# First layer's variance summed with tokens on partitions, its inverse root taken on four columns and spread by a product with a scaled identity

## The chip, the cores and the metric

The kernel runs on one core of a Trainium2 chip. A core has TensorE (matmuls, with the loads of their stationary operand shown apart as PEld), VectorE (DVE), ScalarE (ACT) and GpSimd (POOL); the queue of SyncE (SP) issues all of this kernel's transfers. The metric is the device time of one execution in microseconds (us), as the median of several runs.

## The reference, cut to what matters

Two layers over 1024 tokens of 1024 channels. The change lies in the first one, a convolution module:

```python
h = x @ w_in + b_in
a, a_gate, z = split(h, 3)
u = conv(a * sigmoid(a_gate), width 31, causal, per channel) + b_dw
u = silu(layer_norm(u, ln_g, ln_b))        # over the channels of a token
y = (u * silu(z)) @ w_out + b_out
x = layer_norm(alpha * x + y, g, b)
```

Here `layer_norm` subtracts the mean over the 1024 channels, and multiplies by `rsqrt(var + 1e-5)`, with one variance for each token. The second layer is a dilated sliding-window attention over 16 heads in three groups, with an output projection and a norm of the same kind.

## The kernel before

The kernel is written as steps, each with an engine, a cost, a priority, the steps that it comes after, and buffers that it takes and frees. A planner (`Order.run`) simulates the engines with these costs, takes on each engine the ready step of the smallest priority, and writes all instructions in the order that comes out; each engine then works its own list strictly in that order. So a changed cost can change the written order of every engine from there on, the attention's too.

In the first layer channels lie on the partitions. A tile is 128 channels by 512 tokens; there are eight chunks of channels (0 to 7) and two halves of the tokens (0 and 1). TensorE computes the projections `pa`, `pg` and `pz` (line 300) as three products of split operands. The convolution (`conv`) is a chain of 31 taps for each chunk and half: ScalarE multiplies and GpSimd adds some ten of them (lines 428 and 432, through the tiles `cvt` in the rings `tb0` and `tb1` of two buffers each), VectorE does the others (line 444). VectorE's order is given by `DVE_ORDER`: `c` and `d` are the convolution of half 0 and half 1, `s` is a half's sums (`stats`), `m` what follows them (`apply`).

```python
DVE_ORDER = "c0d0 c1c2 d1c3 c4d2 c5c6 d3c7 s0 m0 d4d5 d6d7 s1 m1".split()
```

`stats` works on one half. The mean over channels is a product with `ones`, a 128x128 matrix whose elements are all 1/1024, so that each partition of the bank `mp` holds the same row of 512 means (line 469). VectorE subtracts it in place (line 483), ScalarE squares (line 488), GpSimd adds some squares in pairs (line 495), and TensorE sums them into the bank `vp`, again with `ones` (line 503): four sums in half 0 (`SUMS` is 8, all in pairs), six in half 1. ScalarE takes the root (line 519) and VectorE the reciprocal (line 523), both on 128x512 and in place. `apply` multiplies each chunk by the result (line 535), and goes on with the activation (line 539), the gate (line 545) and the split for the output projection (lines 550 and 555). The splits of the weights are steps of ScalarE (`whi`, line 241) and of GpSimd or VectorE (`wlo`, line 250), with two buffers each.

The output projection `po` (line 655) takes half 0 and then half 1. What it gives is normalized, turned by TensorE (`pt`, line 799) and split by ScalarE and VectorE (`x1h`, `x1l`, line 815), and becomes the input of the attention. Lines 746 and 750 are the root and the reciprocal on one column in that norm. Lines 935 and 936 are the attention's scores, line 1026 a small product of its softmax.

Of the kernel before, what the change touches and what calls it, by code (L numbers as in the profile page):

```python
# [10 lines left out]
F32 = mybir.dt.float32  # L11
F32R = mybir.dt.float32r
AF = mybir.ActivationFunctionType
OP = mybir.AluOpType

P = 128
D = 1024
# [8 lines left out]
EPS = 1e-5  # L26
# [109 lines left out]
def block_kernel(ctx: ExitStack, tc: tile.TileContext, x, xT, a_w_in, a_vec, a_w_out, rows,  # L136
                 w_k, w_q, w_z, w_v1, w_v23, w_v2, b_w_out, cst, dist, out, dbg=None):
    nc = tc.nc
    consts = ctx.enter_context(tc.tile_pool(name="consts", bufs=1))
# [4 lines left out]
    small = ctx.enter_context(tc.tile_pool(name="small", bufs=2))  # L144
# [10 lines left out]
    order = Order(dict(raw=2, whi=2, wlo=2, pj=4, av=2, cv=2, b4=6, tb0=2, tb1=2, hp=26, gh=2, gl=2, hw=4, xt=4, bias=2))  # L155

    def on(eng, cost, prio, after=(), **kw):
        return lambda fn: order.add(eng, cost, fn, prio, after, **kw)
# [4 lines left out]
    def load(dst, src):  # L163
        return nc.sync.dma_start(dst, src)
# [10 lines left out]
    def tp(name, i, dt=F32):  # L175
        return temp.tile([P, 512], dt, name=name, tag=f"tb{i}")
# [4 lines left out]
    def bank(name, tag, bufs=2):  # L181
        return psum.tile([P, 512], F32, name=name, tag=tag, bufs=bufs)
# [8 lines left out]
    ident, ones, fold = (cs[:, i, :] for i in range(3))  # L191
# [4 lines left out]
    ln_g = av[:, 280:288]  # L196
    ln_b = av[:, 288:296]
    quarter = av[:, 296:300]
    eps = consts.tile([P, 1], F32, name="eps")
    dst = consts.tile([P, GROUPS, 256], F32, name="dst")  # L200
    order.add("dve", 0.05, lambda: nc.vector.memset(eps, EPS), (0, 0))
    vec_in = order.add("dma", 0.4, lambda: load(av, a_vec), (1, 0.9))
    cst_in = order.add("dma", 0.4, lambda: load(cs, cst), (1, 1.9))
    dst_in = order.add("dma", 1.1, lambda: load(dst, dist), (1, 30))
# [3 lines left out]
    def step_no(what):  # L208
        count[what] += 1
        return count[what] - 1  # L210
# [250 lines left out]
    def mean_of(h, y, last):  # L461
        b = mean[h]
        summed[h].append(y)

        @on("pe", 0.86, (0, 0), [last, cst_in] + ([b.last] if b.first else h * [var[0].first]), take=None if b.first else "av", late=MEAN_LATE)
        def mm(start=b.first is None, stop=len(summed[h]) == KT):
            if start:
                b.t = bank("mp", "av")
            nc.tensor.matmul(b.t, lhsT=ones, rhs=y.t, start=start, stop=stop)
        b.first, b.last = b.first or mm, mm  # L470

    def stats(h, idx):

        b = var[h]
        for c in range(KT):
            mean_of(h, Y[c, h], Y[c, h].done)

        def square(c):
            y, q, i = Y[c, h], Box(), step_no("temp") % 2

            @on("dve", 0.6, (1, idx), [mean[h].last], frees=[mean[h].first])
            def center():
                nc.vector.tensor_sub(y.t, y.t, mean[h].t)

            @on("act", 0.52, (0, 2), [center], take=f"tb{i}")
            def sq():
                q.t = tp("sq", i)
                nc.scalar.activation(q.t, y.t, AF.Square)
            q.first = q.last = sq
            return q  # L490

        def join(q, q2):
            @on("pool", 1.22, (0, 2), [q.last, q2.last], frees=[q2.first])
            def plus():
                nc.gpsimd.tensor_add(q.t, q.t, q2.t)
            q.last = plus

        def total(q, end):
            @on("pe", 0.86, (0, 1), [q.last] + ([b.last] if b.first else []), take=None if b.first else "av", frees=[q.first])
            def mm(start=b.first is None):  # L500
                if start:
                    b.t = bank("vp", "av")
                nc.tensor.matmul(b.t, lhsT=ones, rhs=q.t, start=start, stop=end)
            b.first, b.last = b.first or mm, mm

        held = None
        for c in range(KT):
            q = square(c)
            if c < SUMS[h] and held is None:
                held = q  # L510
                continue
            if held:
                join(held, q)
                q, held = held, None
            total(q, c == KT - 1)

        @on("act", 0.55, (0, 2), [b.last], table="sqrt")
        def root():
            nc.scalar.activation(b.t, b.t, AF.Sqrt, bias=eps)

        @on("dve", 3.26, (0.5, 0), [root])
        def inverse():
            nc.vector.reciprocal(b.t, b.t)
        b.last = inverse

    UA = {}
# [1136 lines left out]
```

## Time and profile before

| what | value |
|---|---|
| median of 3 runs | 1667.19 us (1665.12 to 1667.45) |
| profiled execution | 1665.4 us |
| span in its profile | 1663.6 us |
| mean granted clock of TensorE | 0.993 |

The span goes from the first to the last instruction in the profile; the execution's own time lies 1.8 us above it. All times of rows count from the span's start. A matmul's busy time holds its way through the array, so that matmuls that follow each other overlap in the records: their rate is read from their starts.

### The profile page before, as it was taken

What the parts mean: (1) busy time and instruction counts of PE and PEld (TensorE: products, weight loads), DVE (VectorE), ACT (ScalarE), POOL (GpSimd) and SP (SyncE); (2) the same over time, 40 slices, a digit from 0 to 9 for tenths busy, and PEclk for the clock granted to TensorE, in tenths of its full rate; (3) what the DMA queues carried; (4) which work ended last, traced back from release to release, by engine and by line L of the source; (5) the groups of instructions that cost most, each with busy time, mean ns of one, the idle gap of its engine ahead of it and who ended that gap; (6) DMA issues with size and microseconds to landing.
All of it is one profiled execution on the core that took longest, in us unless ns stands there. A gap on an engine that the chain in (4) does not pass through costs nothing.

```text
span 1663.6 us, 24127 instructions
## 1 busy us (share of the span) xinstructions
PE 1620.3 (97%) x8756; PEld 1376.8 (83%) x8756; DVE 1037.0 (62%) x2289; ACT 868.6 (52%) x1962; POOL 901.8 (54%) x514
## 2 busy tenths in 40 slices
PE   8999999988999999999999999999999999999997
PEld 6888877776789888888888888898888889888986
DVE  7999999886663654265465436546644664753448
ACT  6555665364228525543772544387264429527623
POOL 5989996678433446844435673343244434445434
PEclk9999999999999999999999999999999999999999
DMA  5111112543111111311301241130123013013833
GB/s 195 39 51 51 46 55 91 177 146 133 63 41 38 39 39 64 134 45 39 114 26 39 76 132 34 39 114 26 39 89 126 26 51 110 32 39 127 303 115 114
DMA packets 52440, 135.48 MB, mean 81 GB/s; under 512 B 5472, under 2 KB 6752, under 8 KB 52320
## 3 DMA queue, kind: packets, MB, share of 16 engines
q1 hardware_dynamic: 52320, 133.93, 24.0%
q8 instruction: 69, 1.13, 0.3%
q14 instruction: 51, 0.42, 0.1%
HBM read 109.80 MB, written 24.12 MB: 80 GB/s over the span
## 4 chain that ended last, share of the span: by engine, by line
PE 49%; ACT 4%; DVE 1%; issue 1%; POOL 0%; DVEq 0%; POOLq 0%; ACTq 0%
PE pq L300 11%; PE pk L300 10%; PE po L655 5%; PE pv L1219 5%; PE pv L1168 5%; PE pzb L300 4%; PE ptp L1293 3%; PE ps L935 2%; PE ps L936 2%; PE av L1312 1%; PE av L1309 1%; ACT s L1084 1%; ACT ph L1298 0%; ACT s L1075 0%; ACT L1075 0%
## 5 line engine op out<-in xcount | busy, mean ns | idle before, releaser
L243 POOL TENSOR_SCALAR whi<-wraw 128x1024 fp32r<-128x1024 f32 x92 | 257.8, 2802 | 448.2 <-issue 124.3
L250 POOL TENSOR_TENSOR wlo<-wraw,whi 128x1024 fp32r<-128x1024 f32 (+1 forms) x115 | 265.6, 2312 | 85.6 <-ACT whi L241 71.3
L444 DVE SCALAR_TENSOR_TENSOR cva<-u,av,cva 128x512 f32<-128x512 f32 x328 | 222.4, 747 | 0.9
L891 DVE TENSOR_TENSOR kl<-pk,kd 64x512 fp32r<-64x512 f32 x192 | 132.2, 689 | 103.5 <-ACT kd L887 53.3
L432 POOL TENSOR_TENSOR y<-y,cvt 128x512 f32<-128x512 f32 x132 | 170.1, 1310 | 13.5 <-ACT cvt L428 10.2
L1303 DVE TENSOR_TENSOR pl<-ptp,ph 128x384 fp32r<-128x384 f32 (+1 forms) x192 | 109.7, 588 | 103.0 <-ACT ph L1298 98.2
L300 PE MATMUL pk<-x1h,whi 128*128 128x512 f32 x384 | 155.5, 405 | 0.0
L300 PE MATMUL pq<-x1h,whi 128*128 128x512 f32 x384 | 155.0, 404 | 0.0
L939 DVE CUSTOM_DVE_ANT_0 s<-ps,bias 128x256 f32<-128x256 f32 (+1 forms) x384 | 122.8, 371 | 50.9 <-PE ps L936 48.4
L300 PE MATMUL pk<-x1h,wlo 128*128 128x512 f32 x384 | 150.6, 392 | 2.6 <-DVE wlo L250 1.6
L300 PE MATMUL pq<-x1h,wlo 128*128 128x512 f32 x384 | 150.3, 391 | 0.0
L300 PE MATMUL pk<-x1l,whi 128*128 128x512 f32 x384 | 150.3, 391 | 0.0
L300 PE MATMUL pq<-x1l,whi 128*128 128x512 f32 x384 | 150.0, 391 | 0.0
L921 ACT ACTIVATE qs<-pq 64x512 fp32r<-64x512 f32 x96 | 56.9, 592 | 156.8 <-PE pq L300 155.4
L887 ACT ACTIVATE kd<-pk 64x512 fp32r<-64x512 f32 x96 | 56.8, 592 | 146.2 <-PE pk L300 144.6
L1298 ACT ACTIVATE ph<-ptp 128x384 fp32r<-128x384 f32 (+1 forms) x192 | 95.0, 514 | 50.4 <-PE ptp L1293 39.6
L1084 ACT ACTIVATE s<-s,nm 128x128 f32<-128x128 f32 (+1 forms) x256 | 114.0, 463 | 0.0
L428 ACT ACTIVATE cvt<-u,av 128x512 f32<-128x512 f32 x132 | 91.0, 717 | 44.0 <-POOL y L432 43.3
L926 DVE TENSOR_TENSOR qs<-pq,qs 64x512 fp32r<-64x512 f32 x96 | 66.1, 688 | 75.2 <-ACT qs L921 72.8
L1168 PE MATMUL pv<-whi,x1b 128*128 128x256 f32 x512 | 96.2, 287 | 4.4 <-ACT x1b L1133 2.8
L935 PE MATMUL ps<-kd,qs 128*128 128x256 f32 (+1 forms) x384 | 94.8, 280 | 2.5 <-DVE op L1445 1.2
L936 PE MATMUL ps<-kl,qs 128*128 128x256 f32 (+1 forms) x384 | 95.1, 279 | 0.0
(183 smaller groups left out, 4376.5 us busy)
## 6 DMA issues: line engine op xcount, KB each, us to landing
wraw<-in_w_v_dram SPq DMA_DIRECT2D x36, 512.0 KB, 3.4
wraw<-in_w_k_dram SPq DMA_DIRECT2D x24, 512.0 KB, 3.3
wraw<-in_w_q_dram SPq DMA_DIRECT2D x24, 512.0 KB, 3.3
wraw<-in_a_w_in_dram SPq DMA_DIRECT2D x22, 512.0 KB, 3.3
wraw<-in_a_w_out_dram SPq DMA_DIRECT2D x16, 512.0 KB, 3.4
wraw<-in_b_w_out_dram SPq DMA_DIRECT2D x16, 512.0 KB, 3.6
v_d<-v SPq DMA_DIRECT2D x24, 256.0 KB, 2.1
v<-v_d SPq DMA_DIRECT2D x24, 256.0 KB, 5.4
```

The costliest lines, as they stand in the source:

```text
L243: nc.gpsimd.tensor_scalar(self.hi[:, s], self.raw[:, s], 1.0, None, op0=OP.mult)
L250: eng.tensor_sub(self.lo[:, s], self.raw[:, s], f32(self.hi[:, s]))
L300: nc.tensor.matmul(b.t, lhsT=u[:, k, :], rhs=v[h][:, k, :], start=k == 0 and i == 0, stop=k == KT - 1 and i == 2)
L432: nc.gpsimd.tensor_add(y.t, y.t, q.t)
L444: nc.vector.scalar_tensor_tensor(y.t if s == TAPS - 1 and not merged else o.t, src, wc, y.t if s == n_pool else o.t, op0=OP.mult, op1=OP.add)
L891: nc.vector.tensor_sub(d, src, f32(views(g, h, b, own, o.kd[i], own)[0]))
L935: nc.tensor.matmul(ps, lhsT=o.qs[i][:, q], rhs=o.kd[i][:, k], start=True, stop=False)
L936: nc.tensor.matmul(ps, lhsT=o.qs[i][:, q], rhs=o.kl[i][:, k], start=False, stop=True)
L939: nc.vector.tensor_tensor_reduce(s, ps, bias, op0=OP.add, op1=OP.max, scale=1.0, scalar=NEG, accum_out=acc)
L1084: nc.scalar.activation(s, s, AF.Exp, scale=SCALE, bias=a.nm2[:, 2 * i + n, r:r + 1], accum_out=a.d23[:, g - 1, i, n, r:r + 1])
L1168: nc.tensor.matmul(o, lhsT=cols((X1.hi, X1.lo)[u], u, kk), rhs=w[:, kk, :], start=k == 0 and m == 0 and t % 2 == 0, stop=k == KT - 1 and m ...
L1303: nc.vector.tensor_sub(o.pl[:, :n * P], o.t[:, :n * P], f32(o.ph[:, :n * P]))
```

## The change

The variance is summed with tokens on the partitions: each sum becomes four matmuls with 128 tokens of the squares as the stationary operand, and one column of `ones` as the moving one; they fill four columns of the bank, and four columns of 128 tokens hold the variances of a half. ScalarE takes the root of 128x4, with `scale` and a second constant `eps4` such that the result is the root divided by 1024. VectorE takes the reciprocal of 128x4 and multiplies the identity by each of the columns, which gives four diagonal matrices in one 128x512 tile `diag` (it takes a buffer of `tb0` in half 0 and of `tb1` in half 1). A product of `ones` with that tile (`spread`) writes each token's value to all partitions of the same bank; the factor 1/1024 in `ones` takes out the one in the root. `apply` now comes after `spread`. The planner's costs are 0.2 for the root, 0.8 for VectorE's step, and 0.86 for the spread; the cost of each sum stays.

```diff
@@ -196,9 +196,10 @@
     ln_g = av[:, 280:288]
     ln_b = av[:, 288:296]
     quarter = av[:, 296:300]
-    eps = consts.tile([P, 1], F32, name="eps")
+    eps, eps4 = consts.tile([P, 1], F32, name="eps"), consts.tile([P, 1], F32, name="eps4")
     dst = consts.tile([P, GROUPS, 256], F32, name="dst")
     order.add("dve", 0.05, lambda: nc.vector.memset(eps, EPS), (0, 0))
+    order.add("dve", 0.05, lambda: nc.vector.memset(eps4, EPS / D ** 2), (0, 0))
     vec_in = order.add("dma", 0.4, lambda: load(av, a_vec), (1, 0.9))
     cst_in = order.add("dma", 0.4, lambda: load(cs, cst), (1, 1.9))
     dst_in = order.add("dma", 1.1, lambda: load(dst, dist), (1, 30))
@@ -500,7 +501,9 @@
             def mm(start=b.first is None):
                 if start:
                     b.t = bank("vp", "av")
-                nc.tensor.matmul(b.t, lhsT=ones, rhs=q.t, start=start, stop=end)
+                for j in range(4):
+                    nc.tensor.matmul(b.t[:, j:j + 1], lhsT=q.t[:, j * P:(j + 1) * P], rhs=ones[:, 0:1],
+                                     start=start and j == 0, stop=end and j == 3, skip_group_check=True)
             b.first, b.last = b.first or mm, mm
 
         held = None
@@ -514,13 +517,22 @@
                 q, held = held, None
             total(q, c == KT - 1)
 
-        @on("act", 0.55, (0, 2), [b.last], table="sqrt")
+        @on("act", 0.2, (0, 2), [b.last], table="sqrt")
         def root():
-            nc.scalar.activation(b.t, b.t, AF.Sqrt, bias=eps)
-
-        @on("dve", 3.26, (0.5, 0), [root])
+            b.sd = small.tile([P, 4], F32, name="sd4")
+            nc.scalar.activation(b.sd, b.t[:, 0:4], AF.Sqrt, bias=eps4, scale=float(D) ** -2)
+
+        @on("dve", 0.8, (0.5, 0), [root], take=f"tb{h}")
         def inverse():
-            nc.vector.reciprocal(b.t, b.t)
+            nc.vector.reciprocal(b.sd, b.sd)
+            b.diag = tp("diag", h).rearrange("p (j t) -> p j t", j=4)
+            nc.vector.tensor_tensor(b.diag, ident[:, None, :].broadcast_to([P, 4, P]),
+                                    b.sd[:, :, None].broadcast_to([P, 4, P]), op=OP.mult)
+
+        @on("pe", 0.86, (0, 0), [inverse], frees=[inverse])
+        def spread():
+            nc.tensor.matmul(b.t, lhsT=ones, rhs=b.diag.rearrange("p j t -> p (j t)"), start=True, stop=True)
+        inverse = spread
         b.last = inverse
 
     UA = {}
```

## Rows read from the trace of the kernel before

**Rows 1.** The page: busy time by engine, and the granted clock in 40 slices.
```profile
PE 1620.3 (97%) x8756; PEld 1376.8 (83%) x8756; DVE 1037.0 (62%) x2289; ACT 868.6 (52%) x1962; POOL 901.8 (54%) x514
...
PEclk9999999999999999999999999999999999999999
```

**Rows 2.** Windows: from:to, length, busy us (xinstructions) per engine, clock, DMA share, GB/s.
```profile
0.00:20.00 20.00, 15.11 (x52) 11.10 (x53) 10.84 (x21) 13.04 (x24) 7.75 (x12) 1.00 0.86 283
200.00:340.00 140.00, 138.45 (x570) 106.63 (x569) 126.94 (x174) 75.82 (x108) 105.40 (x69) 1.00 0.33 109
340.00:424.00 84.00, 72.75 (x314) 56.56 (x313) 63.44 (x97) 41.23 (x65) 65.22 (x37) 0.92 0.41 137
```

**Rows 3.** Groups by line and shape: busy us, mean ns | idle ahead, releaser.
```profile
L555 DVE TENSOR_TENSOR ul<-y,uh 128x512 fp32r<-128x512 f32 x16 | 16.7, 1089 | 1.1 <-ACT uh L550 1.1
...
L503 PE MATMUL vp<-sq,cs 128*128 128x512 f32 x20 | 9.8, 603 | 0.8 <-POOL sq L495 0.7
...
L523 DVE RECIPROCAL vp<-vp 128x512 f32<-128x512 f32 x2 | 6.7, 3356 | 6.7 <-ACT vp L519 6.7
...
L503 PEld LDWEIGHTS vp<-sq,cs 128*128 128x128 f32 x20 | 3.6, 189 | 4.3 <-POOL sq L495 2.1 <-issue 1.9
...
L746 ACT ACTIVATE sd<-mv,eps 128x1 f32<-128x1 f32 x12 | 2.8, 284 | 10.5 <-DVE mv L741 10.5
...
L750 DVE RECIPROCAL sd<-sd 128x1 f32<-128x1 f32 x12 | 1.9, 156 | 1.1 <-ACT sd L746 0.9
...
L519 ACT ACTIVATE vp<-vp,eps 128x512 f32<-128x512 f32 x2 | 1.3, 662 | 1.5 <-PE vp L503 1.5
```

**Rows 4.** TensorE in order of time, 322 to 328 us: start, us, what, xcount.
```profile
322.90 0.39 PE L655 MATMUL po<-wlo,uh 128*128 128x512 f32 x1
323.13 4.45 PE L503 MATMUL vp<-sq,cs 128*128 128x512 f32 x10
...
327.65 0.39 PE L655 MATMUL po<-whi,ul 128*128 128x512 f32 x1
```

**Rows 5.** Who TensorE waited for, 340 to 424 us: total us, times, longest.
```profile
PE pt L799 <- DVE x1l L815: 7.5, 7, 2.3
PE po L655 <- POOL wlo L250: 2.0, 2, 1.8
...
PE po L655 <- ACT whi L241: 0.7, 1, 0.7
```

**Rows 6.** Weight loads in order of time, 1025 to 1026 us, short score matmuls.
```profile
1025.19 0.19 PEld L936 LDWEIGHTS ps<-kl,qs 128*128 128x128 f32 x1
...
1025.41 0.19 PEld L936 LDWEIGHTS ps<-kl,qs 128*128 128x128 f32 x1
```

**Rows 7.** TensorE in order of time, 502.7 to 503.4 us, matmuls of 64 columns.
```profile
502.88 0.33 PE L1026 MATMUL sw<-wide,cs 128*128 128x64 f32 x2
503.02 0.49 PE L1168 MATMUL pv<-whi,x1b 128*128 128x256 f32 x2
```

**Rows 8.** VectorE in order of time, 240 to 330 us.
```profile
239.80 6.01 DVE L444 SCALAR_TENSOR_TENSOR cva<-u,av,cva 128x512 f32<-128x512 f32 x9
245.73 3.35 DVE L523 RECIPROCAL vp<-vp 128x512 f32<-128x512 f32 x1
```

**Rows 9.** VectorE in order of time, 326.5 to 332.5 us.
```profile
328.31 3.37 DVE L523 RECIPROCAL vp<-vp 128x512 f32<-128x512 f32 x1 [6.66 <-ACT vp L519]
331.71 1.29 DVE L535 TENSOR_TENSOR y<-y,vp 128x512 f32<-128x512 f32 x2
```

**Rows 10.** Windows of 4 us, columns as in rows 2.
```profile
344.00:348.00 4.00, 1.50 (x6) 0.70 (x5) 4.00 (x5) 2.96 (x5) 3.63 (x3) 1.00 0.00 0
348.00:352.00 4.00, 4.00 (x13) 3.15 (x12) 4.00 (x5) 0.63 (x1) 2.30 (x1) 0.63 0.60 165
```

**Rows 11.** TensorE in order of time, 349 to 350 us.
```profile
349.06 0.63 PE L655 MATMUL po<-wlo,uh 128*128 128x512 f32 x1
349.49 0.63 PE L655 MATMUL po<-whi,uh 128*128 128x512 f32 x1
```

## The prediction

> **What bounds the kernel now.** Read first the table of engines and the clock line on the profile's page [rows 1]: TensorE is busy for 97% of the span, and its granted clock is full in almost every slice. So a microsecond saved on another engine comes out of the total only where TensorE waits for that engine, while a microsecond of TensorE's own work is paid in full. Next the busy time by stage [rows 2]: while the convolution and the two normalizations run (200 to 340 us) TensorE is busy 138.45 of 140 us and VectorE 126.94; from 340 to 424 us TensorE is busy only 72.75 of 84 at a mean clock of 0.92. So the cover lies in the first stage, and what can be won or lost by waiting lies in the second, directly behind the second half's normalization. Then the groups of the lines that the diff touches [rows 3], and TensorE's order of time around the second half's sums [rows 4]: projection matmuls come 0.23 us apart, then ten variance matmuls, then projection again. Last, who TensorE waits for in that second stage [rows 5].
>
> **TensorE's work, removed and added.** The trace has 20 matmul instructions on the variance line for ten sums (four in half 0, six in half 1), so a 32-bit matmul is two instructions here, each with its own weight load [rows 3]. From 323.13 to 327.65 us lie ten of them and one projection matmul of 0.23: (4.52 - 0.23) / 10 = 0.43 us each [rows 4]. Removed: 20 x 0.43 = 8.6 us.
>
> Added: each sum becomes four products with one moving column, so 10 x 4 x 2 = 80 matmuls, and 80 loads of 128x128 weights, since now the squares are the weights. No row shows one moving column with these loads. The nearest are the short score matmuls, where loads of 128x128 start 1025.19 and, two later, 1025.41 us: 0.11 us apart, although 128 columns in one pass leave little else to do [rows 6]. I take 0.11, because this row is bound by the same thing, the load: 80 x 0.11 = 8.8 us. From below, two matmuls of 64 columns took 0.14 us together, 0.07 each, with part of their loads hidden behind their neighbours [rows 7]: 5.6 us. From above, one load recorded 0.19 us [rows 3], and if none overlapped it would be 15.2 us.
>
> The page "TensorE: Matmul & The Clock Gate" of the Trainium skill gives, in "Back-to-back issue gap", some 60 cycles for a matmul of up to 64 columns, with a floor near 25 ns; my estimate from it alone is 80 x 0.025 = 2.0 us and a saving of almost 5 us in all. Its section on LDWEIGHTS prices a load by its 128 columns (107 ns), and on that one the trace agrees with 0.11 us.
>
> Then the spread: two products with 512 columns, 2 x 2 x 0.43 = 1.7 us. TensorE's sum: 8.8 + 1.7 - 8.6 = +1.9 us; with the low price -1.3, with the high one +8.3. The change thus exchanges twenty long matmuls for eighty loads that take as long, and pays for the spread besides.
>
> **VectorE and ScalarE.** The reciprocal of 128x512 took 3.36 us, twice [rows 3]. In its place stand a reciprocal on four columns, for which the one on a single column, 0.16 us, is the nearest row, and a 128x512 product of identity and column. That product reads two operands from SBUF; the nearest such rows are the splits of line 555, mean 1.09 us [rows 3]. Saved: 3.36 - 0.16 - 1.09 = 2.1 us in each half. ScalarE's root falls from 0.66 us to some 0.28, that of a root on one column [rows 3]. The constant for the root adds one memset of one column at the start, where VectorE is busy 10.84 of 20 us [rows 2]: nothing, or below 0.2 us.
>
> In half 0 the 2.1 us is really VectorE's: the reciprocal starts at 245.73 us directly behind nine convolution taps of 6.01 us [rows 8], and the engine is nearly full up to the end of the convolution. So half 1's sums can start up to 2.1 us sooner. TensorE however has projections to do all that time, so this alone is worth nothing to the end. In half 1 VectorE stood idle for 6.66 us ahead of the reciprocal; from its start to the first normalization is 331.71 - 328.31 = 3.4 us [rows 9]. In the new order these 3.4 us become 0.16 + 1.09 for the two VectorE steps, 0.86 for the spread and about 0.6 for it to drain and to be seen (one matmul is recorded with 0.60 us [rows 3]): 2.7 us, with 0.4 from the root. Half 1's normalization then starts about 1 us sooner by the chain and 2 by VectorE, 3 in all.
>
> The diagonal takes one of two buffers in a ring that the convolution's products on ScalarE use too. It is held some 2 us in half 0; GpSimd's taps could wait that long. VectorE's own taps and TensorE's projections cover that; without them it would cost the 2 us.
>
> **The new wait.** Until now TensorE waited for nothing between the last sum and the output projection. Now the spread waits in its queue for VectorE, and behind it stand the gate projections (half 0) or the output projection (half 1); ScalarE's activations and the weight splits wait for those. The written order puts the spread where the planner expects the diagonal. If VectorE is on time this costs nothing, since the work ahead covers the chain. If VectorE is behind by a long operation, I bound it by one product, 1.1 us in each half. I take 0.5 us for both, and give the relief of the second stage the same 0.5, so the two cancel.
>
> **Sum.** Profiled execution 1665.4 us (span 1663.6 and 1.8 around it) + 1.9 = 1667.3. The median of the runs shown is 1.8 higher than this execution, which makes 1669.1 on that footing. I put the time between them: 1668.2 us.
>
> **Rivals.** *The second stage is relieved (faster).* TensorE waits there 7.5 us for VectorE at the transposes and 2.7 us for the splits of the output weights [rows 5]. Around 347 us ScalarE's queue is full with half 1's activations; TensorE is busy 1.50 of 4 us, and then the clock falls to 0.63 in the next stretch [rows 10], where matmuls come 0.43 us apart instead of 0.23 [rows 11]: eight of them lose 1.6 us. If half 1's work comes 3 us sooner, that wait and this fall can go: 2.7 + 1.6 = 4.3 us, and part of the transposes' 7.5. Time: 1668.2 - 4.3 = 1664, down to 1661. Against it: most of the 7.5 us lies at the transposes, and VectorE's order there is planned anew too, with the same optimistic costs.
>
> *The clock falls behind the short matmuls (slower).* In half 1 five sums stand in one run [rows 4]; they become forty matmuls of one column, 40 x 0.11 = 4.4 us in which the array multiplies almost nothing. The trace shows the clock at full through today's run, and the fall of this stage behind a stretch in which TensorE did little, at 344 to 348 us [rows 10]. If the new run counts as little, the price is that of the fall at 349 us, 1.6 us, and up to as much again for loads at half clock. It decides from 1.4 us on, since 1.9 + 1.4 passes the bound of 0.2%: 1670 to 1672 us. "The HAM clock gate" of the same page of the Trainium skill says that the half rate is the state after idleness, and that activity releases it; by that rule the result hangs on whether a one-column matmul is activity. No row here can tell.
>
> *The spread waits (slower).* If VectorE is late in half 0, where it is full, by two taps and more, TensorE stands for 1.5 to 3 us: 1670 to 1671. For it speaks that VectorE has no slack; against it, that TensorE has projections ahead of the spread.
>
> *The load price is off.* At 0.07 us the kernel comes to 1665; at 0.19 to 1674 or 1675.5.
>
> **How the numbers follow.** Forecast (work +1.9, waits cancel) 0.43; relief 0.20; clock 0.17; waiting spread 0.10; load price low 0.04, high 0.06. Three runs of before spread over 0.14%, so 0.2%, 3.3 us, is about what can be told from no change. Faster takes the relief and a little of the low price, 0.22; slower takes most of clock and spread, the high price, and a tail of the forecast, 0.30; within 0.2% is 0.48. The range goes from a full relief, 1660.5, to the high price of the loads, 1675.5; the forecast's own range is 1665 to 1670.5.
>
> **What would show it.** In the changed profile: 80 matmuls on the variance line 0.11 us apart; VectorE without the 3.36 us reciprocals; half 1's normalization some 3 us sooner against the sums; 340 to 424 us with waits of like size. Wrong would be: clock below 1 directly behind the run of short matmuls; TensorE waiting at the spread; the wait for the output weights near 347 us gone; or new waits far behind, in the attention, because the written order was planned anew.

## The result, and the profile after

The changed kernel takes 1674.85 us (median of 4 runs, 1674.27 to 1676.83), the kernel before 1666.7: a ratio of 1.0061 with a 95% interval of 1.0048 to 1.0073, 8 us slower by the medians. (Ratios here and below are those on record; they are not exactly the quotient of two medians, which is 1.0049 here.) The forecast was 1668.2 us and no measurable change.

First the page of the changed kernel, then its windows, against [rows 1] and [rows 2].

```profile
PE 1624.6 (97%) x8820; PEld 1384.1 (83%) x8820; DVE 1033.6 (62%) x2292; ACT 867.3 (52%) x1962; POOL 902.1 (54%) x514
```

```profile
200.00:340.00 140.00, 135.09 (x586) 107.54 (x585) 117.61 (x174) 74.06 (x106) 96.19 (x64) 0.95 0.27 89
340.00:424.00 84.00, 74.53 (x330) 58.14 (x329) 61.97 (x86) 38.98 (x61) 68.58 (x38) 0.98 0.44 150
```

TensorE's busy time grew by 4.3 us, the span from 1663.6 to 1672.5. The stage that the prediction took for covered is the one that lost: from 200 to 340 us TensorE is busy 135.09 us instead of 138.45, and its mean clock is 0.95 instead of 1.00. The stage behind it, where relief was looked for, looks no worse in this view, 74.53 us busy and 0.98, but by then the kernel is some 8 us late, so that the window holds other work.

When each kind of matmul begins and ends says where the time went. The view by tile gives counts, shortest, median and longest duration in ns, and the first and last start in us. First the changed kernel, for the gate's projections, the output projection and the attention's scores, then the kernel before.

```profile
L301 PE MATMUL pz<-xh,whi x128: 386/390/803, 192.7 to 299.9; 128*128 128x512 f32 x128
...
L667 PE MATMUL po<-whi,uh x128: 387/392/800, 300.6 to 412.4; 128*128 128x512 f32 x128
...
L947 PE MATMUL ps<-kd,qs x384: 220/279/388, 440.0 to 1513.1; 128*128 128x256 f32 x112, 128*128 128x128 f32 x80
```

```profile
L300 PE MATMUL pz<-xh,whi x128: 389/389/798, 192.8 to 292.0; 128*128 128x512 f32 x128
...
L655 PE MATMUL po<-whi,uh x128: 390/393/797, 292.7 to 402.1; 128*128 128x512 f32 x128
...
L935 PE MATMUL ps<-kd,qs x384: 219/279/387, 428.9 to 1504.2; 128*128 128x256 f32 x112, 128*128 128x128 f32 x80
```

The gate's projections begin alike (192.7 and 192.8 us) and end 7.9 us late. The last output projection of the first layer starts 10.3 us late, the scores 11.1 us. From there on nothing more is lost: the last scores are 8.9 us late, as the end of the span is. So all of it is lost between 192 and 440 us: 7.9 us while the gate is projected, 3.2 up to the scores, and in the attention 2 us come back.

TensorE in the gate's stage of the changed kernel, in order of time (in brackets how long an instruction waited, and for what):

```profile
258.83 0.39 PE L301 MATMUL pz<-xh,wlo 128*128 128x512 f32 x1
261.71 0.50 PE L301 MATMUL pz<-xh,whi 128*128 128x512 f32 x1 [2.49 <-ACT whi L242]
...
264.16 0.80 PE L301 MATMUL pz<-xh,wlo 128*128 128x512 f32 x1 [1.71 <-POOL wlo L251]
264.75 0.63 PE L301 MATMUL pz<-xh,whi 128*128 128x512 f32 x1
265.18 0.63 PE L301 MATMUL pz<-xl,whi 128*128 128x512 f32 x1
```

It has a next projection to start at 259.06 us, 0.23 behind the last, and starts it at 261.71, for want of the weight's first part; the second part comes at 264.16. Then the clock is at half: matmuls 0.43 us apart (264.75, 265.18). Before, no projection waited there. The first part is made by ScalarE. Its list in order of time, changed kernel first, then the kernel before:

```profile
251.22 2.92 ACT L551 ACTIVATE y<-y,av 128x512 f32<-128x512 f32 x4
...
260.04 0.67 ACT L380 ACTIVATE z<-pz,av 128x512 f32<-128x512 f32 x1
260.61 2.00 ACT L242 ACTIVATE whi<-wraw 128x1024 fp32r<-128x1024 f32 x2
```

```profile
248.15 1.05 ACT L241 ACTIVATE whi<-wraw 128x1024 fp32r<-128x1024 f32 x1
...
250.27 2.23 ACT L539 ACTIVATE y<-y,av 128x512 f32<-128x512 f32 x3 [0.46 <-DVE y L535]
```

Before, the split (`whi`, line 241) ran at 248.15 us, ahead of the activations of half 0 that begin at 250.27. In the changed kernel the activations begin right behind the gate's, at 251.22, and two splits stand at 260.61, behind all eight of half 0's. The diff touches none of these instructions; the planner wrote them in this order from the lower costs.

### The profile page after: what moved, and what is told of

The parts are those of the page before. It is cut to its first block, busy times and chain, and to the rows that moved or that the text cites. A ratio compares the mean times of both kernels' runs of the same rounds, so it can differ in the third digit from the quotient of the medians.

```text
span 1672.5 us, 24257 instructions
## 1 busy us (share of the span) xinstructions
PE 1624.6 (97%) x8820; PEld 1384.1 (83%) x8820; DVE 1033.6 (62%) x2292; ACT 867.3 (52%) x1962; POOL 902.1 (54%) x514
## 4 chain that ended last, share of the span: by engine, by line
PE 48%; ACT 5%; DVE 1%; issue 1%; POOL 1%; DVEq 0%; POOLq 0%; ACTq 0%
PE pq L301 11%; PE pk L301 10%; PE po L667 5%; PE pv L1231 5%; PE pzb L301 4%; PE pv L1180 3%; PE ptp L1305 2%; PE ps L947 2%; PE ps L948 2%; ACT s L1096 2%; PE av L1324 1%; PE av L1321 1%; ACT x1b L1145 1%; ACT s L1087 1%; ACT ph L1310 1%
```

## The experiments

Each line gives the median and the ratio to the kernel before, run on the same chip, with its interval. The kernel before came to 1665.71 us beside e1 to e4, 1663.98 beside e5 to e8, and 1664.53 beside e9 to e12.

**Work and order taken apart (e1, e2).** e1 keeps the changed instructions and gives the planner the old costs, which gives nearly, not exactly, the old order:

```diff
-        @on("act", 0.2, (0, 2), [b.last], table="sqrt")
+        @on("act", 0.55, (0, 2), [b.last], table="sqrt")
...
-        @on("dve", 0.8, (0.5, 0), [root], take=f"tb{h}")
+        @on("dve", 0.8, (0.5, 0), [root])
...
+        rest = order.add("dve", 2.46, lambda: None, (-1, 0), [inverse])
-        @on("pe", 0.86, (0, 0), [inverse], frees=[inverse])
+        @on("pe", 0.0, (0, 0), [inverse])
...
-        inverse = spread
-        b.last = inverse
+        b.last = rest
```

> The changed instructions, written in nearly the order of the kernel before: the planner is given the old costs (0.55 for the root, 3.26 for the step of the reciprocal, nothing for the spread). Theory of the order (the loss comes from the splits of the gate's weights, which the new plan puts behind half 0's activations on ScalarE, so that TensorE stands at 259 to 264 us and its clock falls): that wait is gone, 1667 to 1670 us, with what the clock takes behind the short matmuls still in it. Theory of the work (the short matmuls, their clock and the spread are the loss themselves): 1674 us as in the changed kernel.

e2 keeps the old instructions and gives the planner the changed costs (0.2 and 0.8, the buffer of the ring, and a step of 0.86 on TensorE that issues nothing; the memset of `eps4` is issued too).

> The instructions of the kernel before, written in the order of the changed one: the planner is given the changed costs, the instructions stay. Theory of the order: the wait at the gate's weights near 260 us appears here too, 1671 to 1674 us. Theory of the work: no difference from the kernel before, 1666 to 1668 us.

Measured: e1 1671.29 us, 1.0031 (1.0020 to 1.0042). e2 1674.97 us, 1.0059 (1.0047 to 1.0071): the old instructions in the new order are as slow as the changed kernel (1.0061), without one new matmul. So the order alone is enough for the whole loss. But e1 shows that the work, in nearly the old order, costs 5.6 us too, above the expected range of 1667 to 1670; both theories had a part. The two don't add up, and TensorE and ScalarE of e2 show why:

```profile
256.20 0.39 PE L301 MATMUL pz<-xh,wlo 128*128 128x512 f32 x1
261.90 0.79 PE L301 MATMUL pz<-xh,whi 128*128 128x512 f32 x1 [5.31 <-ACT whi L242]
```

```profile
260.80 1.99 ACT L242 ACTIVATE whi<-wraw 128x1024 fp32r<-128x1024 f32 x2
```

ScalarE's splits run at 260.80 us here and at 260.61 in the changed kernel: that time is set by ScalarE. TensorE arrives at 256.43 here and waits 5.3 us; in the changed kernel it arrives 2.6 us later and waits 2.5. So what its added work and clock took ahead of the wait, the wait gave back; that is read from these two profiles, and not tested by itself.

**The clock (e3, e4).** e3 is the changed kernel with 128 moving columns, e4 the same in e1's order.

```diff
-                    nc.tensor.matmul(b.t[:, j:j + 1], lhsT=q.t[:, j * P:(j + 1) * P], rhs=ones[:, 0:1],
+                    nc.tensor.matmul(b.t[:, j * P:(j + 1) * P], lhsT=q.t[:, j * P:(j + 1) * P], rhs=ones,
...
-            nc.scalar.activation(b.sd, b.t[:, 0:4], AF.Sqrt, bias=eps4, scale=float(D) ** -2)
+            nc.scalar.activation(b.sd, b.t.rearrange("p (j t) -> p j t", j=4)[:, :, 0], AF.Sqrt, bias=eps4, scale=float(D) ** -2)
```

> The changed kernel with 128 moving columns of ones instead of one in each product of the sums, so that the same 80 weight loads stand beside products that keep the array at work; the root reads every 128th column. Theory of the clock (one-column matmuls count as idleness, so the clock falls behind their runs near 238 and 327 us): both falls vanish and the kernel gains 1.7 to 3.4 us against the changed one, 1671.5 to 1673. Rival (the falls come from other idleness, or the price is the loads alone): both falls stay, 1674 to 1676.

> Both edits together: 128 moving columns, and the order of the kernel before. If order and clock are the two parts of the loss, what is left is TensorE's added work of 1.9 us at most: 1666 to 1669 us, and no fall of the clock between 200 and 340 us. If they are not, it stays above 1671.

Measured: e3 1673.47 us, 1.0047 (1.0035 to 1.0060), 1.4 us below the changed kernel; the two intervals overlap, so a difference is not shown. e4 1667.82 us, 1.0016 (1.0008 to 1.0025), 3.5 us below e1; here the intervals touch, but six of e1's seven runs (1670.63 to 1672.09) lie above all eleven of e4 (1666.92 to 1669.91). The windows around the two runs of sums, changed kernel first, then e3 (the clock is the figure behind POOL's):

```profile
236.00:244.00 8.00, 7.83 (x39) 6.67 (x40) 8.00 (x13) 6.21 (x10) 7.17 (x6) 0.79 0.01 2
322.00:334.00 12.00, 12.00 (x62) 9.94 (x61) 5.93 (x11) 3.72 (x5) 4.35 (x4) 0.86 0.14 45
```

```profile
236.00:244.00 8.00, 7.56 (x40) 6.11 (x38) 7.80 (x13) 7.03 (x12) 7.81 (x7) 1.00 0.01 2
322.00:334.00 12.00, 12.00 (x62) 9.85 (x61) 8.36 (x16) 6.24 (x9) 3.57 (x2) 1.00 0.21 71
```

The clock is 0.79 and 0.86 there with one moving column, and full with 128: the falls went, as the theory said, while its gain of 1.7 to 3.4 us is not shown. TensorE's order of time in e1 and then in e4, at half 1's run of forty matmuls, with e1's window ahead:

```profile
300.00:340.00 40.00, 40.00 (x180) 32.69 (x180) 26.68 (x42) 11.47 (x15) 25.45 (x16) 0.91 0.43 148
```

```profile
326.66 6.07 PE L505 MATMUL vp<-cs,sq 128*128 128x1 f32 x40
332.60 0.77 PE L668 MATMUL po<-whi,uh 128*128 128x512 f32 x1
333.17 0.63 PE L668 MATMUL po<-whi,ul 128*128 128x512 f32 x1
333.60 0.63 PE L668 MATMUL po<-wlo,uh 128*128 128x512 f32 x1
```

```profile
326.26 4.63 PE L505 MATMUL vp<-cs,sq 128*128 128x128 f32 x40
330.65 0.48 PE L668 MATMUL po<-whi,uh 128*128 128x512 f32 x1
```

With 128 columns forty matmuls take 330.65 - 326.26 = 4.39 us, 0.11 each. With one column the same forty take 5.94 us, since the clock falls in the middle of the run, and the projection behind is at 0.43 us per matmul up to 336.41: 1.6 us in the run and as much behind it, 3.2 in all, near the 3.5 between the medians. (Of the two profiles themselves 2.7 us of difference lie ahead of the gate's projections, before any sum, so the spans are not compared.)

One moving column does not make the clock fall each time. Half 1 in e5, a run described below, has the same sixteen and then thirty-two short matmuls as the changed kernel, with the same six projections between them:

```profile
320.40 3.63 PE L505 MATMUL vp<-cs,sq 128*128 128x1 f32 x32
...
324.67 0.39 PE L667 MATMUL po<-whi,uh 128*128 128x512 f32 x1
324.90 0.39 PE L667 MATMUL po<-whi,ul 128*128 128x512 f32 x1
```

Here the projections behind are 0.23 us apart, and the clock is 1.00 from 322 to 334 us. Half 0's short matmuls in e1 and e5 left it full too (1.00 from 236 to 244 us). What decides is not shown. In the profiles with 128 columns (e3, e4, e7, e11) no fall stands behind the sums.

The thirty-two of e5 take 3.48 us up to the next projection at 323.88, 0.11 each, as with 128 columns: 128 times the arithmetic costs no time here. That the clock is the difference between e1 and e4 is shown. But e4's expectation of no fall at all between 200 and 340 us missed: from 268 to 300 us its clock is 0.95. Among its waits (200 to 440 us; total, times, longest) the first has grown from 0.7 us and the second is new, both for VectorE; e1 has the same two, at full clock there:

```profile
PE mp L470 <- DVE y L445: 1.8, 1, 1.8
PE vp L536 <- DVE diag L529: 1.2, 1, 1.2
```

**The split put first (e5, e7, e11), the changed kernel.** e5 alters one priority; e7 adds the 128 columns; e11 adds a truer planned cost of the first norm's gain (1.7; in e7 its eight instructions on VectorE take 1.78 us in the median).

```diff
-            @on(hi_eng, hi_cost, (0.5, n), [fetch] + ([self.home.slot] if self.home else []), take=None if i or self.home else "whi")
+            @on(hi_eng, hi_cost, (0, 1.5, n) if hi_eng == "act" else (0.5, n), [fetch] + ([self.home.slot] if self.home else []), take=None if i or self.home else "whi")
...
-                ("dve", 1.2, nc.vector) if v == "d" else ("pool", 1.67, nc.gpsimd) for v in path)
+                ("dve", 1.7, nc.vector) if v == "d" else ("pool", 1.67, nc.gpsimd) for v in path)
```

> The changed kernel, with one priority altered: the plan takes ScalarE's part of a weight split ahead of half 0's and half 1's activations instead of behind them. Nothing is computed otherwise. Theory of the order (the loss is that split, late behind an unbroken run of activations): TensorE's wait for it near 260 us goes, and the kernel comes to 1666 to 1670 us, with the clock's falls behind the short matmuls still in it. Rival (the plan's shift costs in many places, and this split is only the one that is seen): 1672 to 1676.

> The altered priority and 128 moving columns in the sums, in the changed kernel. Order and clock both mended: 1664 to 1667 us, the level of the kernel before or a little below, the added work of TensorE (below 2 us) left. If it stays above 1670, a third cause is missing.

> The changed kernel with 128 columns and the splits first, and the plan's cost of the first norm's gain on VectorE raised from 1.2 to the 1.7 us that a busy GpSimd makes of it, so that the transposes are written later. If what is left of the loss is TensorE standing at transposes written too early (its clock fell near 369 us): 1665 to 1668 us. If not: 1671 or more, as without it.

Measured: e5 1673.6 us, 1.0054 (1.0041 to 1.0067); e7 1671.7 us, 1.0039 (1.0027 to 1.0051); e11 1667.98 us, 1.0019 (1.0009 to 1.0028). So e5's theory fell in the form in which it was put: the one split is not the whole loss of the order. By its own expectation e7, above 1670, says that a third cause is missing. Windows of e5, and TensorE at the transposes:

```profile
240.00:268.00 28.00, 27.03 (x122) 21.90 (x121) 27.69 (x35) 23.80 (x36) 24.29 (x17) 1.00 0.16 57
364.00:384.00 20.00, 14.35 (x64) 11.61 (x63) 17.49 (x17) 8.57 (x14) 18.67 (x12) 0.74 0.44 157
```

```profile
372.05 1.94 PE L811 MATMUL pt<-cs,rx 128*128 128x128 f32 x8 [3.93 <-DVE x1l L827]
```

The wait for the gate's split is gone: 27.03 us busy of 28 at full clock, where the changed kernel has 23.80 at 0.87. But from 364 to 384 us TensorE is now busy 14.35 us of 20 at a clock of 0.74, standing 3.93 us at a transpose for VectorE. At the transposes it waits 10.4 us in all, against 7.6 in the changed kernel. So part of what the first stage gave, the second took. This profile is of e5's fastest run, 1670.24 us against a median of 1673.6, so what the other runs lost besides is not seen. e11's windows:

```profile
240.00:268.00 28.00, 26.98 (x118) 21.69 (x117) 27.69 (x36) 22.98 (x34) 24.29 (x17) 1.00 0.16 57
364.00:384.00 20.00, 16.75 (x74) 12.68 (x73) 17.47 (x22) 8.47 (x14) 18.80 (x12) 0.83 0.44 158
```

With the transposes planned later the second stretch comes to 16.75 us at 0.83, and the median lies 3.7 us below that of e7, run on another chip (1.0019 against 1.0039, the intervals touching at 1.0027 to 1.0028). That the transposes make this gain is not shown: in the two profiles the scores begin at 433.0 us (e7) and 433.1 (e11), with new waits of TensorE ahead of them. With these mends 3.5 us above the kernel before are left (1667.98 against 1664.53).

**The same mends in the kernel before (e6, e12), and VectorE's time alone (e8).** e6 has the priority of e5, e12 the cost of e11, each in the kernel before. e8 shortens the reciprocal and leaves the rest of the bank without it:

```diff
-            nc.vector.reciprocal(b.t, b.t)
+            nc.vector.reciprocal(b.t[:, 0:4], b.t[:, 0:4])
```

> The kernel before with the same altered priority. Its own wait for the output weights near 345 us (2.5 us, and a fall of the clock of 1.6) has the same pattern, so by the theory of the order it shrinks: 1662 to 1665 us against some 1666. If the gate's splits in half 0 are all there is to it, no change.

> The kernel before with that planned cost of 1.7 us alone. It waits 7.5 us at the transposes between 340 and 424 us. If a truer cost mends that: 1660 to 1663 us, better than both kernels. If waits only move: 1664 to 1668.

> The kernel before in its own order, with the reciprocal taken on four of the 512 columns only; the rest of the bank is left as the root, so the values of the normalization are not those of the reference. It takes 3.2 us off VectorE in each half and alters nothing else. If VectorE's saved time is worth nothing to the end, as the prediction said: 1665 to 1667 us, like the kernel before. If it relieves the second stage: 1661 to 1664.

Measured: e6 1665.32 us, 1.0003 (0.9995 to 1.0012); e12 1664.62 us, 1.0004 (0.9995 to 1.0013); e8 1664.41 us, 1.0002 (0.9994 to 1.0011). No difference is shown in any. The kernel before gains nothing that can be told from either mend, nor from 3.2 us less of VectorE in each half. None of the twelve is shown to be faster than it.

**Only the planned cost (e9, e10).** The instructions of the kernel before, with another planned cost of its reciprocal: 2.6 in e9, 2.0 in e10.

```diff
-        @on("dve", 3.26, (0.5, 0), [root])
+        @on("dve", 2.0, (0.5, 0), [root])
```

> The instructions of the kernel before; only the plan's cost of the reciprocal is lowered from 3.26 to 2.6 us. In this order the gate's split still stands ahead of half 0's activations. If the late split alone makes the loss of the order: no wait at 260 us and 1664 to 1667 us, like the kernel before. If a shifted plan costs at several places (the second stage above all): 1668 us or more without that wait.

> The same with 2.0 us: now the split stands behind the activations, as in the changed kernel. Both theories: a wait for the gate's split near 260 us, and 1670 to 1675 us. If it stays at 1666, the wait is not the cause even there.

Measured: e9 1668.24 us, 1.0018 (1.0009 to 1.0027); e10 1675.68 us, 1.0060 (1.0048 to 1.0073). In e9 the split still stands ahead of the activations. Its windows, with the second one of the kernel before behind them, then its wait for the output weights:

```profile
240.00:268.00 28.00, 28.00 (x124) 22.82 (x123) 27.44 (x33) 24.96 (x37) 25.20 (x18) 1.00 0.17 57
340.00:352.00 12.00, 8.94 (x29) 6.83 (x30) 6.43 (x14) 5.08 (x7) 5.14 (x2) 0.72 0.26 87
```

```profile
340.00:352.00 12.00, 9.49 (x34) 7.02 (x33) 12.00 (x13) 7.38 (x12) 7.78 (x4) 0.88 0.20 55
```

```profile
PE po L655 <- ACT whi L241: 2.8, 1, 2.8
```

The gate's stage is whole (28 of 28 us). From 340 to 352 us TensorE is busy 8.94 us of 12 at 0.72, against 9.49 at 0.88 before, with a wait of 2.8 us for a split of the output weights (0.7 before, [rows 5]). So the profile shows a loss in the second stage; whether it is all that the median lost is not shown, since the profiled run, 1666.69 us, is one of e9's fastest. In e10 the split stands behind the activations, and TensorE waits for it:

```profile
PE pz L300 <- ACT whi L241: 2.1, 1, 2.1
```

Between 2.6 and 2.0 us of planned cost lie 7.4 us of time, with not one instruction different. Of e9's two theories the second held: there is no wait at the gate's split and still 1668 us, so a shifted plan costs 3 to 4 us elsewhere. With the late split, in e10, it costs as much as the whole change (1.0060).

## Why the prediction was wrong, point by point

**What bounds the kernel** was right in its outline: TensorE's time and waits are what counts. e8 bears it out: with VectorE's 3.2 us a half taken away and the order kept, no difference is shown.

**TensorE's work** was sized well. The groups of the changed kernel, against [rows 3]:

```profile
L505 PE MATMUL vp<-cs,sq 128*128 128x1 f32 x80 | 9.5, 247 | 0.2 <-POOL sq L496 0.2
...
L529 DVE TENSOR_TENSOR diag<-cs,sd 128x512 f32<-128x512 f32 x2 | 1.4, 705 | 0.3 <-DVE sd L527 0.2
...
L527 DVE RECIPROCAL sd<-sd 128x4 f32<-128x4 f32 x2 | 0.3, 167 | 0.0
...
L523 ACT ACTIVATE sd<-vp,eps 128x4 f32<-128x4 f32 x2 | 0.5, 263 | 3.3 <-PE vp L505 3.3
```

There are 80 matmuls, at 0.11 us each at full clock (3.48 us for thirty-two in e5), as taken from [rows 6]. The Trainium skill's "TensorE: Matmul & The Clock Gate" has the same in its LDWEIGHTS section (its formula gives 107 ns for 128 columns). The estimate of 0.025 us from "Back-to-back issue gap" is refuted by that 0.11; the section itself calls such a figure the isolated gap of a single matmul, which at few columns leaves out the weight load. With a new weight for each, one column and 128 take the same time here, so the load sets the pace. The diagonal took 0.71 us, not 1.09, and the root 0.26, not 0.28. e4, the changed work with the clock kept and nearly the old order, is 2.1 us above the kernel before, against the +1.9 of the sum; its interval goes from 1.3 to 4.2 us, and it has new waits besides, so that the match is in part luck.

**The sum's missing term is the written order.** The step that failed stands in the part on VectorE: "TensorE however has projections to do all that time". That VectorE's time is worth nothing was right; what failed is that the projections were taken as ready in the new order too. Each needs a split from ScalarE, and ScalarE's list changes with the plan: half 0's normalization comes sooner in the plan, its activations have the better priority, and the split falls behind nine microseconds of them (251.22 to 260.04 us). The prediction named a plan made anew only as a last doubt, far behind in the attention, and gave it no price. e2 gives it: the old instructions in the new order come to 1.0059, all of the loss; e9 and e10 show that the plan's number alone does it. One place is seen in the profile, the gate's split: TensorE stands 2.5 and 1.7 us there, and the clock falls behind. It is not the whole, since e5, without that wait, is not shown to be faster than the changed kernel (1.0054 against 1.0061); what the order costs in the second stage is seen in e5, e9 and e11 and not priced place by place. The measured 1674.85 us lies inside the outer range, which ends at 1675.5, by luck: that end stands for loads at 0.19 us, and they took 0.11.

**The relief of the second stage** did not come. VectorE's head start was taken to reach half 1. The chain there, against [rows 9]:

```profile
328.55 0.69 DVE L685 SCALAR_TENSOR_TENSOR rx<-rx,po 128x512 f32<-128x512 f32 x1 [4.06 <-PE po L667]
329.15 0.17 DVE L527 RECIPROCAL sd<-sd 128x4 f32<-128x4 f32 x1
...
333.30 1.88 DVE L547 TENSOR_TENSOR y<-y,vp 128x512 f32<-128x512 f32 x3
```

ScalarE ran the root from 326.46 to 326.72 us; the reciprocal began at 329.15, behind an addition of line 685 that waited 4.06 us for the output projection, and the normalization at 333.30, not 331.71. The prediction wanted it 3 us sooner against the sums. Counted from the first projection behind them, at 327.02 us before (the line below) and 326.28 now, it came after 4.7 us before and comes after 7.0 now. In VectorE's list the reciprocal has work of another chain ahead of it, and in TensorE's list the spread stands behind output projections. A chain of four engines has a queue at each of them; the prediction priced the operations and the hops, and no queue. Where the relief was brought about, it was worth nothing that can be told: in e6 the wait near 347 us is gone (TensorE is busy all 24 us from 340 to 364 at full clock, 21.50 at 0.93 before), and the scores begin at 428.9 us in both.

```profile
327.02 0.79 PE L655 MATMUL po<-whi,uh 128*128 128x512 f32 x1
```

**The clock rival** was right in its place and price. The run of half 1 in the changed kernel, against [rows 4]:

```profile
322.79 3.63 PE L505 MATMUL vp<-cs,sq 128*128 128x1 f32 x32
326.28 0.48 PE L667 MATMUL po<-whi,uh 128*128 128x512 f32 x1
...
327.81 0.63 PE L667 MATMUL po<-wlo,uh 128*128 128x512 f32 x1
328.24 0.63 PE L667 MATMUL po<-whi,uh 128*128 128x512 f32 x1
```

Behind thirty-two short matmuls the projection comes 0.43 us apart (327.81, 328.24). The forecast price was 1.6 us and up to as much again; e4 against e1 measured 3.5 us. The prediction could not tell whether the clock would fall behind one-column matmuls. It fell, from 2.4 to 1.2 GHz, in both halves of the changed kernel and in half 1 of e1; it held in half 0 of e1 and in both halves of e5, and behind the same sums with 128 columns in e3 and e4.

**The wait of the spread** was taken as 0.5 us, cancelled by relief. Where the clock had not fallen ahead of it, as in e4, TensorE waited 1.2 us for the diagonal in half 0; in the changed kernel no wait for it shows, since TensorE came later. This rival was real and small.

What stays open: the 3.5 us that e11 still lies above the kernel before are not taken apart; TensorE's added work (1.9) is in them, the rest is argued from waits alone. Open too is which places of the new order make its loss besides the gate's split, and why the clock falls behind the same short matmuls in one run and not in another.

## What to carry to other kernels

Where a planner writes the instruction lists from costs, a changed cost is an edit to every list: run the old instructions in the new order, and the new ones in the old order, before the operations themselves are judged. On the engine that bounds, ask of each stretch that is called cover what the work in it waits for, and whether that supply has moved. A matmul with the operands exchanged is priced by its weight loads, and if it has one moving column it may cost the clock as well; widening the moving operand to 128 columns took no more time here, since the load hides it.

## What the runs showed of the hardware

Behind or within runs of 32 and 40 matmuls with one moving column TensorE's clock fell to half in two profiles, although TensorE was recorded busy without a gap (12.00 of 12 us at 0.86 in the changed kernel, 40.00 of 40 at 0.91 in e1): its busy share in the profile is no sign that the clock will hold. In a third, e5, it held at 1.00 behind the same 32. With 128 columns, the same loads and the same 0.11 us per matmul, it held in all four.
